# A hybrid attention and convolution trunk in float32: q, k and v projected 512 columns at a time, bias and scale at eviction

## The chip, the cores and the metric

The kernel runs on one core of one Trainium2 chip. The metric is the device time of one execution in microseconds, the median of three. In the profile PE is TensorE's matmul, PEld its weight load, DVE VectorE, ACT ScalarE, POOL GpSimd and SP SyncE. Line numbers such as L332 are those of the kernel before; the order lists of the changed kernel carry its own numbers.

## The reference, cut

Two layers over a sequence of 512 tokens of width 1024, all in float32. Each is a feed-forward half step, the mixer, a second feed-forward half step and a norm. The change lies in the mixer:

```python
def mixer(h, ...):
    z = h @ w_in + b_in
    q, k, v, glu_in, gates = jnp.split(z, [1536, 3072, 4608, 6656], axis=-1)
    shp = (B, S, 3, 8, 64)              # 3 groups of 8 heads of 64
    q = apply_rope(rmsnorm(q.reshape(shp), q_norm[:, None, :]), cos, sin)
    k = apply_rope(rmsnorm(k.reshape(shp), k_norm[:, None, :]), cos, sin)
    v = v.reshape(shp)
    for g, (window, dil) in enumerate(((128, 1), (512, 4), (2048, 16))):
        o, l = dilated_window_attn(q[:, :, g], k[:, :, g], v[:, :, g], dil, window // (2 * dil))
    ...                                  # groups weighted by softmax of l, projected
    y_conv = conv_module(glu_in, ...)    # GLU, depthwise conv of 31, LayerNorm, silu, projection
    g_attn, g_conv = jnp.split(jax.nn.sigmoid(gates), 2, axis=-1)
    return (g_attn * y_attn + g_conv * y_conv) @ w_out
```

## The kernel before

Every float32 product is made of three matmuls on operands split into their upper and lower 12 bits: upper by upper, upper by lower, lower by upper (L166 to L168, where a helper issues them). `stage` (L155 to L164) fetches weights by SP into a raw tile of [128, 1024] (512 KB, two buffers), ScalarE casts the upper part (`hi`, L161) and VectorE subtracts for the lower (`lo`, L162); hi and lo have four buffers each. Activations are kept split too, transposed, as xgh and xgl: eight tiles of [128 channels, 512 tokens], not yet divided by the row norm.

The mixer computes the GLU's input (ps_ga, ps_gg into u), then for each of three head groups and each of two halves of four heads: a chunk of 256 columns of q, one of k, one of v, and the attention of these heads (scores ps_S, transposed probabilities ps_T, output ps_pv). Then come the gates (ps_gc, ps_gA, 192 matmuls each), the depthwise convolution, its LayerNorm, and the projections ps_cp, of the attention, and of the output. The convolution is one multiplication (L543) and 30 multiply-adds (L549) on VectorE for each of eight channel tiles, 240 multiply-adds a layer. The LayerNorm takes the sum of the eight tiles (L555), its mean by a matmul with ones (ps_mu, L557), a copy (L559), eight subtractions (L562), squares (L193) and their sums (L197, ps_ss L202), the root (L207), a diagonal (L216) broadcast by ps_bc (L218), then multiplication (L567), Silu (L568) and a new split (zh L175, zl L176), whose tiles ps_cp reads.

`tokens_chunk` (L320 to L337) projects 256 columns with tokens on the partitions: two stages of four row blocks, and for each of four token tiles eight row blocks by three matmuls of 128x256 (L332 to L334) and a fourth kind (L336) that adds the bias: a row of three parts of the bias against a row of three parts of 1/r (rt3, made at L286 to L297, ps_rt at L291), since the division by the row norm r comes later. There are 18 chunks a layer. For q and k, ScalarE copies the two PSUM banks out (z, L374), squares 64 columns at a time with an accumulator (L377, 16 for each chunk), VectorE rotates (L379 to L381) and normalizes (small operations on [128, 16], L383 to L390), TensorE transposes (ps_qT) and ScalarE copies into qkT (L401). v is scaled by ScalarE at eviction (L412) and goes through DRAM to its order of positions.

A scheduler sets the order of each engine's instructions when the program is built; each engine works its list in order. `stage` is ranked 150 places early, and the LayerNorm is ranked ahead of the attention. PSUM has eight banks: two named mm (projections), one st, five at (attention, transposes). The pools of the mixer hold four qkT pairs and ten V tiles.

Of the kernel before, what the change touches and what calls it, by code (L numbers as in the profile page):

```python
# [32 lines left out]
CH = 256            # columns of q, k or v at a time: four heads  # L33
# [11 lines left out]
def trunk(ctx: ExitStack, tc: tile.TileContext, A: dict, out: bass.AP):  # L45
# [8 lines left out]
    def ps_mm(name):  # L54
        return psp.tile([P, S], F32, tag="mm", name=name, bufs=2)
# [17 lines left out]
    # input, natural layout  # L73
# [153 lines left out]
    def proj_cols(src, c0, rhs, nk, ps):  # L227
        """ps[j] = src[:, c0 + 128 j ..].T @ rhs, one or two tiles of columns."""
# [44 lines left out]
    def mixer(l, xg, R, rc, after):  # L273
# [5 lines left out]
        with ExitStack() as mx:  # L279
# [5 lines left out]
            # 1 / r as a row of three parts, and eps / r^2  # L285
            rr, rt = rc  # L286
            e4 = rp.tile([P, TT], F32, tag="e4", name=uniq("e4"))
            nc.vector.scalar_tensor_tensor(e4, rt, EPS, rt, op0=ALU.mult, op1=ALU.mult)
            ps = ps_st(uniq("ps_rt"))
            for tt in range(TT):  # L290
                nc.tensor.matmul(ps[:1, tt * P:(tt + 1) * P], rt[:, tt:tt + 1], ident, start=True, stop=True)  # L291
            rh, rl_ = slot("tmp", 7, F32R)[:1, :], slot("tmp", 7, F32R)[:1, :]
            nc.scalar.activation(rh, ps[:1, :], AF.Copy)
            nc.vector.tensor_sub(rl_, ps[:1, :], rh.bitcast(F32))
            rt3 = slot("rt3", 1, F32R)[:3, :]
            for i, t in enumerate((rh, rl_, rh)):
                nc.gpsimd.dma_start(rt3[i:i + 1, :], t)  # L297

# [487 lines left out]
```

## Time and profile before

| | |
|---|---|
| three runs | 2724.01, 2725.06, 2725.06 us |
| median | 2725.06 us |
| profiled execution, span from first to last instruction | 2723.4 us |
| TensorE matmul busy in it | 2704.4 us (99%), 14013 instructions |
| VectorE busy | 1536.0 us (56%) |
| ScalarE busy | 1148.1 us (42%) |
| GpSimd busy | 149.6 us (5%) |
| granted TensorE clock, mean | 0.998 |

Busy times are of one execution, and the profile gives that execution no time beside its span. A matmul's row lasts longer than the distance to the next one, as matmuls are pipelined; the distance is read from start times. Instructions of VectorE overlap a little in the same way. A share of the whole span says little here, since the mixers (about 471 to 887 us, and 1819 to 2234 us) load VectorE quite otherwise than the feed-forward steps.

### The profile page before, as it was taken

To read this page: it belongs to the slowest core of one execution; us is meant where nothing else is said; L and a number is where in the kernel's file an instruction comes from. 1 tells how busy PE (TensorE), PEld (TensorE's weight loads), DVE (VectorE), ACT (ScalarE), POOL (GpSimd) and SP (SyncE) were. 2 spreads that over 40 slices of the span, in tenths; PEclk is the share of its full clock that TensorE was granted. 3 is DMA by queue.
4 is the path that set the end of the run, shared out by engine and by line. 5 is a ranking of instruction groups with operands and counts; after the bars stand their busy time and mean duration, and the time that the engine had idled before them with its cause. 6 is when DMAs were issued, how large, how long until landed. Compare 5 with 4: busy or idle time off the path is not lost.

```text
span 2723.4 us, 35608 instructions
## 1 busy us (share of the span) xinstructions
PE 2704.4 (99%) x14013; PEld 2242.8 (82%) x14013; DVE 1536.0 (56%) x2543; ACT 1148.1 (42%) x2457; POOL 149.6 (5%) x275
## 2 busy tenths in 40 slices
PE   8999999999999999999999999999999999999998
PEld 6888888988887788888888888889888877888887
DVE  4443344888888754443454434458888876434432
ACT  5232232656677343232333222335567773322322
POOL 2000000111120000000000000001111200000000
PEclk9999999999999999999999999999999999999999
DMA  4232233223233323322333333322322333333322
GB/s 157 93 101 91 93 98 94 88 87 98 86 101 104 123 89 98 100 93 93 93 94 100 94 95 94 99 91 87 96 86 87 106 107 116 93 101 93 101 89 74
DMA packets 260455, 264.50 MB, mean 97 GB/s; under 512 B 12542, under 2 KB 251742, under 8 KB 260288
## 3 DMA queue, kind: packets, MB, share of 16 engines
q1 hardware_dynamic: 247488, 234.91, 27.9%
q0 software_dynamic: 12784, 27.32, 3.3%
q8 instruction: 110, 1.80, 0.3%
q14 instruction: 57, 0.47, 0.1%
q10 hardware_dynamic: 16, 0.00, 0.0%
HBM read 247.18 MB, written 14.99 MB: 96 GB/s over the span
## 4 chain that ended last, share of the span: by engine, by line
PE 97%; ACT 1%; DVE 1%; DMA 0%; issue 0%; SPq 0%; ACTq 0%
PE ps_n L332 6%; PE ps_d L167 6%; PE ps_d L166 6%; PE ps_d L168 6%; PE ps_a L167 6%; PE ps_b L166 6%; PE ps_a L168 6%; PE ps_b L168 6%; PE ps_b L167 6%; PE ps_a L166 6%; PE ps_n L333 5%; PE ps_n L334 5%; PE ps_n L336 2%; PE ps_pv L487 2%; PE ps_S L457 1%; PE ps_T L479 1%
## 5 line engine op out<-in xcount | busy, mean ns | idle before, releaser
L162 DVE TENSOR_TENSOR lo<-raw,hi 128x1024 fp32r<-128x1024 f32 (+1 forms) x448 | 539.4, 1204 | 797.1 <-ACT hi L161 795.6
L161 ACT ACTIVATE hi<-raw 128x1024 fp32r<-128x1024 f32 (+1 forms) x448 | 467.7, 1044 | 970.6 <-issue 353.8
L332 PE MATMUL ps_n<-hi,xgh 128*128 128x256 f32 x1152 | 343.5, 298 | 0.0
L549 DVE SCALAR_TENSOR_TENSOR cv<-u,cwc,cv 128x497 f32<-128x497 f32 (+14 forms) x480 | 335.7, 736 | 0.1
L333 PE MATMUL ps_n<-lo,xgh 128*128 128x256 f32 x1152 | 330.1, 287 | 0.0
L334 PE MATMUL ps_n<-hi,xgl 128*128 128x256 f32 x1152 | 328.6, 285 | 0.0
L168 PE MATMUL ps_d<-sh,lo 128*128 128x512 f32 x704 | 277.4, 394 | 0.0
L166 PE MATMUL ps_d<-sh,hi 128*128 128x512 f32 x704 | 277.4, 394 | 0.0
L167 PE MATMUL ps_d<-sl,hi 128*128 128x512 f32 x704 | 277.4, 394 | 0.0
L167 PE MATMUL ps_b<-xgl,hi 128*128 128x512 f32 x704 | 275.5, 391 | 0.0
L167 PE MATMUL ps_a<-xgl,hi 128*128 128x512 f32 x704 | 274.1, 389 | 0.1
L168 PE MATMUL ps_a<-xgh,lo 128*128 128x512 f32 x704 | 274.1, 389 | 0.0
L166 PE MATMUL ps_b<-xgh,hi 128*128 128x512 f32 x704 | 273.9, 389 | 0.0
L168 PE MATMUL ps_b<-xgh,lo 128*128 128x512 f32 x704 | 273.9, 389 | 0.0
L166 PE MATMUL ps_a<-xgh,hi 128*128 128x512 f32 x704 | 273.3, 389 | 0.3 <-ACT xgh L183 0.3
L332 PEld LDWEIGHTS ps_n<-hi,xgh 128*128 128x128 f32 x1152 | 219.4, 190 | 21.4 <-issue 2.8
L333 PEld LDWEIGHTS ps_n<-lo,xgh 128*128 128x128 f32 x1152 | 220.0, 191 | 3.9 <-issue 3.6
L334 PEld LDWEIGHTS ps_n<-hi,xgl 128*128 128x128 f32 x1152 | 219.9, 191 | 2.4 <-issue 2.1
L166 PEld LDWEIGHTS ps_d<-sh,hi 128*128 128x128 f32 x704 | 131.7, 187 | 32.6
L168 PEld LDWEIGHTS ps_d<-sh,lo 128*128 128x128 f32 x704 | 131.6, 187 | 32.6
L167 PEld LDWEIGHTS ps_d<-sl,hi 128*128 128x128 f32 x704 | 131.7, 187 | 32.6
L168 PEld LDWEIGHTS ps_b<-xgh,lo 128*128 128x128 f32 x704 | 132.2, 188 | 28.3 <-issue 1.0
(247 smaller groups left out, 4276.5 us busy)
## 6 DMA issues: line engine op xcount, KB each, us to landing
raw<-in_ffn_w_up_dram SPq DMA_DIRECT2D x176, 512.0 KB, 3.5
raw<-in_w_in_dram SPq DMA_DIRECT2D x136, 512.0 KB, 3.6
raw<-in_ffn_w_down_dram SPq DMA_DIRECT2D x76, 512.0 KB, 3.4
raw<-in_w_conv_proj_dram SPq DMA_DIRECT2D x16, 512.0 KB, 3.4
raw<-in_w_out_dram SPq DMA_DIRECT2D x16, 512.0 KB, 3.5
vd<-tmp POOLq DMA_DIRECT2D x24, 256.0 KB, 2.7
od<-ot POOLq DMA_DIRECT2D x24, 256.0 KB, 3.0
oin<-od POOLq DMA_DIRECT2D x24, 256.0 KB, 3.0
```

Of the source, the lines that this page charges most:

```text
L161: nc.scalar.activation(hi[:, :m], raw[:, :m], AF.Copy)
L162: nc.vector.tensor_sub(lo[:, :m], raw[:, :m], hi[:, :m].bitcast(F32))
L166: nc.tensor.matmul(ps, ah, bh, start=first, stop=False)
L167: nc.tensor.matmul(ps, ah, bl, start=False, stop=False)
L168: nc.tensor.matmul(ps, al, bh, start=False, stop=last)
L332: nc.tensor.matmul(o, xh[:, ts], wh, start=k == 0, stop=False)
L333: nc.tensor.matmul(o, xh[:, ts], wl, start=False, stop=False)
L334: nc.tensor.matmul(o, xl[:, ts], wh, start=False, stop=False)
L336: nc.tensor.matmul(o, rt3[:, ts], b3, start=False, stop=True)
L457: nc.tensor.matmul(pS[e][:, w * n + lo:w * n + hi], qT[hp, i, b * P:(b + 1) * P], kT[hp, i, k0 + lo:k0 + hi], start=True, stop=True)
L487: nc.tensor.matmul(pv[e * 64:(e + 1) * 64, i, b - b2, :], V[b + j][:, h * HD:(h + 1) * HD], PT[e][:, (nj * w + j) * P:(nj * w + j + 1) * P ...
L549: nc.vector.scalar_tensor_tensor(a[:, t0:t1], u[k][:, t0 + d:t1 + d], cw(l, j, k), a[:, t0:t1], op0=ALU.mult, op1=ALU.add)
```

## The change

A chunk is now 512 columns: 256 of q and 256 of k of the same four heads side by side, or 512 of v for a group's eight heads, so nine chunks a layer. It has four stages of two row blocks (for q and k two transfers of 256 KB into each raw tile), and thereby fills all four hi and lo buffers. The matmuls are 128x512, in two passes of two token tiles. The bias matmul, the row 1/r and its three-part tiles are gone: VectorE evicts each bank with one operation, times the row's scale plus the bias, which a POOL transfer has spread over all partitions. Squares are one ScalarE instruction of 128x512 for each token tile, and VectorE sums them by heads. Tables, qkT and the gates' tiles are merged to match; V is loaded for the eight heads of a group at once. PSUM has three mm banks and four at. In a group the two q-and-k chunks come first, then v, then the two halves' attention.

```diff
@@ tile pools
-        return psp.tile([P, S], F32, tag="mm", name=name, bufs=2)
+        return psp.tile([P, S], F32, tag="mm", name=name, bufs=3)
-        return psp.tile([P, S], F32, tag="at", name=name, bufs=5)
+        return psp.tile([P, S], F32, tag="at", name=name, bufs=4)
@@ stage
-            nc.sync.dma_start(raw[:, :m].rearrange("p (a n) -> p a n", a=a), src)
+            rv = raw[:, :m].rearrange("p (a n) -> p a n", a=a)
+            for i, src in enumerate(srcs):
+                nc.sync.dma_start(rv[:, :, i * n1:(i + 1) * n1], src)
@@ tokens_chunk
-                w = [stage(win[:, kk:kk + 4, c0:c0 + CH]) for kk in (0, 4)]
-                b3 = mp.tile([3, CH], F32R, tag="bias", name=uniq("bias"), bufs=2)
-                nc.gpsimd.dma_start(b3, bd[(l * 3 * AW + c0) // CH])
-                for tt in range(TT):
-                    ts = slice(tt * P, (tt + 1) * P)
-                    o = ps[tt // 2][:, (tt % 2) * CH:(tt % 2 + 1) * CH]
+                n = S // len(cols)
+                bias = mp.tile([P, S], F32, tag="bias", name=uniq("bias"), bufs=2)
+                for i, c0 in enumerate(cols):
+                    nc.gpsimd.dma_start(bias[:, i * n:(i + 1) * n], bass.AP(tensor=A["b_in"].tensor, offset=A["b_in"].offset + l * IN_W + c0, ap=[[0, P], [1, n]]))
+                w = [stage(*(win[:, kk:kk + 2, c0:c0 + n] for c0 in cols)) for kk in range(0, KD, 2)]
+                for t2 in range(0, TT, 2):
+                    ps = [ps_mm(uniq("ps_n")) for _ in range(2)]
                     for k in range(KD):
-                        wh, wl = w[k // 4][0][:, k % 4], w[k // 4][1][:, k % 4]
+                        wh, wl = w[k // 2][0][:, k % 2], w[k // 2][1][:, k % 2]
                         xh, xl = xg[k]
-                        nc.tensor.matmul(o, xh[:, ts], wh, start=k == 0, stop=False)
-                        nc.tensor.matmul(o, xh[:, ts], wl, start=False, stop=False)
-                        nc.tensor.matmul(o, xl[:, ts], wh, start=False, stop=False)
-                    # the bias, over the scale that the rows still lack
-                    nc.tensor.matmul(o, rt3[:, ts], b3, start=False, stop=True)
-                return ps
+                        for t in range(2):
+                            ts = slice((t2 + t) * P, (t2 + t + 1) * P)
+                            mm3(ps[t], xh[:, ts], xl[:, ts], wh, wl, k == 0, k == KD - 1)
+                    for t in range(2):
+                        yield t2 + t, ps[t], bias
@@ qk_chunk
-                for i in range(2):
-                    nc.scalar.activation(zt[i], ps[i], AF.Copy)
-                    for t in range(2):
-                        for h in range(UH):
-                            nc.scalar.activation(trash, four(zt[i])[:, t, h], AF.Square, accum_out=v[:, 2 * i + t, h:h + 1])
+                for tt, ps, bias in tokens_chunk((c0, AW + c0)):
+                    z = slot("sgc", 8, name="z")
+                    nc.vector.scalar_tensor_tensor(z, ps, rr[:, tt:tt + 1], bias, op0=ALU.mult, op1=ALU.add)
+                    sq = slot("tmp", 7, name="sq")
+                    nc.scalar.activation(sq, z, AF.Square)
+                    nc.vector.reduce_sum(v[:, tt, :], sq.rearrange("p (h d) -> p h d", d=HD), axis=AX.X)
@@ v_chunk
+                for tt, ps, bias in tokens_chunk((2 * AW + g * AOW,)):
+                    v = slot("tmp", 7)
+                    nc.vector.scalar_tensor_tensor(v, ps, rr[:, tt:tt + 1], bias, op0=ALU.mult, op1=ALU.add)
+                    nc.gpsimd.dma_start(vd[tt * P:(tt + 1) * P, :], v)
@@ the loop over groups
-                tq, tk = tables(g, 0), tables(g, 1)
+                tab = tables(g)
+                qkT = [qk_chunk(g, hh, tab) for hh in range(2)]
+                V = v_chunk(g)
                 for hh in range(2):
-                    qT = qk_chunk(g, hh, 0, tq)
-                    kT = qk_chunk(g, hh, 1, tk)
-                    V = v_chunk(g, hh)
-                    attend(g, hh, qT, kT, V)
+                    attend(g, hh, qkT[hh], V)
```

Three places of the order lists show what moves. On VectorE, early in the first layer's first q chunk, before:

```order
L549 SCALAR_TENSOR_TENSOR cv_7437<-u_2733,cwc,cv_7437 128x498
L549 SCALAR_TENSOR_TENSOR cv_7469<-u_2740,cwc,cv_7469 128x498
L549 SCALAR_TENSOR_TENSOR cv_7437<-u_2733,cwc,cv_7437 128x499
L379 TENSOR_TENSOR p_513_3297<-z_3293,tab_3165 128x8x32
L380 TENSOR_TENSOR p_513_3297<-z_3293,tab_3165 128x8x32
L549 SCALAR_TENSOR_TENSOR cv_7469<-u_2740,cwc,cv_7469 128x499
L549 SCALAR_TENSOR_TENSOR cv_7437<-u_2733,cwc,cv_7437 128x500
```

and VectorE at the same place of the changed kernel, where L516 is the convolution:

```order
L516 SCALAR_TENSOR_TENSOR cv_6198<-u_2707,cwc,cv_6198 128x502
L347 SCALAR_TENSOR_TENSOR z_3230<-ps_n_3180,rsr_2563,bias_3149 128x512
L516 SCALAR_TENSOR_TENSOR cv_6230<-u_2714,cwc,cv_6230 128x502
L347 SCALAR_TENSOR_TENSOR z_3240<-ps_n_3181,rsr_2563,bias_3149 128x512
L516 SCALAR_TENSOR_TENSOR cv_6198<-u_2707,cwc,cv_6198 128x503
L352 TENSOR_TENSOR p_510_3235<-z_3230,tab_3138 128x8x32
L353 TENSOR_TENSOR p_510_3235<-z_3230,tab_3138 128x8x32
L516 SCALAR_TENSOR_TENSOR cv_6230<-u_2714,cwc,cv_6230 128x503
L350 TENSOR_REDUCE ssh_3146<-sq_3232 128x8
```

The evictions of PSUM (L347) and the sums of squares (L350) now stand between the convolution's instructions.

On TensorE, at the end of a chunk and the start of the next, before:

```order
L332 MATMUL ps_n_3348<-hi_3356,xgh_2560 128x256
L333 MATMUL ps_n_3348<-lo_3357,xgh_2560 128x256
L334 MATMUL ps_n_3348<-hi_3356,xgl_2561 128x256
L336 MATMUL ps_n_3348<-bias_3361,rt_401_2600 128x256
L332 MATMUL ps_n_3521<-hi_3524,xgh_1981 128x256
L333 MATMUL ps_n_3521<-lo_3525,xgh_1981 128x256
```

and TensorE at such a place of the changed kernel:

```order
L157 MATMUL ps_n_3251<-hi_3174,xgh_2549 128x512
L158 MATMUL ps_n_3251<-lo_3175,xgh_2549 128x512
L159 MATMUL ps_n_3251<-hi_3174,xgl_2550 128x512
L157 MATMUL ps_n_3389<-hi_3362,xgh_1970 128x512
L157 MATMUL ps_n_3390<-hi_3362,xgh_1970 128x512
L158 MATMUL ps_n_3389<-lo_3363,xgh_1970 128x512
```

The bias matmul is gone, and two token tiles of the new chunk (3389 and 3390) run side by side.

On TensorE, around the broadcast ps_bc of the convolution's LayerNorm, before:

```order
L167 MATMUL ps_gA_7370<-xgl_2371,hi_7404 128x512
L168 MATMUL ps_gA_7370<-xgh_2370,lo_7405 128x512
L218 MATMUL ps_bc_7750<-dg_7745,ones 128x512
L166 MATMUL ps_gA_7370<-xgh_2465,hi_7404 128x512
L167 MATMUL ps_gA_7370<-xgl_2466,hi_7404 128x512
L168 MATMUL ps_gA_7370<-xgh_2465,lo_7405 128x512
L166 MATMUL ps_gA_7371<-xgh_1981,hi_7374 128x512
```

and TensorE there in the changed kernel:

```order
L158 MATMUL ps_gA_6133<-xgl_2550,hi_6165 128x512
L159 MATMUL ps_gA_6133<-xgh_2549,lo_6166 128x512
L193 MATMUL ps_ss_6497<-ones,sq_6467 128x1 x4
L209 MATMUL ps_bc_6511<-dg_6506,ones 128x512
L157 MATMUL ps_cp_6688<-zh_6515,hi_6691 128x512
L157 MATMUL ps_cp_6689<-zh_6515,hi_6691 128x512
L158 MATMUL ps_cp_6688<-zl_6516,hi_6691 128x512
```

The gate's matmuls that stood between the LayerNorm's matmuls and ahead of ps_cp have moved forward, and ps_ss, ps_bc and ps_cp follow one another.

## Rows read from the trace of the kernel before

**Rows 1.** The page: busy time (1) and the chain that ended last (4).

```profile
PE 2704.4 (99%) x14013; PEld 2242.8 (82%) x14013; DVE 1536.0 (56%) x2543; ACT 1148.1 (42%) x2457; POOL 149.6 (5%) x275
...
PE 97%; ACT 1%; DVE 1%; DMA 0%; issue 0%; SPq 0%; ACTq 0%
```

**Rows 2.** Busy by window: length, PE, PEld, DVE, ACT, POOL, clock, DMA share, GB/s.

```profile
470.90:844.60 373.70, 373.70 (x2708) 325.50 (x2707) 320.73 (x696) 247.59 (x819) 56.84 (x102) 1.00 0.30 91
...
1006.00:1370.00 364.00, 364.00 (x1594) 297.92 (x1593) 150.53 (x177) 113.18 (x140) 0.00 (x0) 1.00 0.31 96
...
1819.00:2192.10 373.10, 373.10 (x2705) 324.92 (x2705) 320.58 (x696) 247.00 (x819) 56.83 (x102) 1.00 0.30 91
```

**Rows 3.** Timeline of PE in the first q chunk: start, length, engine, line, operation.

```profile
471.15 0.28 PE L332 MATMUL ps_n<-hi,xgh 128*128 128x256 f32 x1
...
476.69 0.28 PE L332 MATMUL ps_n<-hi,xgh 128*128 128x256 f32 x1
...
477.29 0.28 PE L334 MATMUL ps_n<-hi,xgl 128*128 128x256 f32 x1
477.49 0.38 PE L336 MATMUL ps_n<-bias,rt 3*128 3x256 f32 x1
477.81 0.39 PE L332 MATMUL ps_n<-hi,xgh 128*128 128x256 f32 x1
```

**Rows 4.** The chain of waits around the row 1/r, layer 1.

```profile
402.35 0.96 PE ps_rt L291 x8
```

**Rows 5.** Timeline of DVE: the LayerNorm's eight subtractions.

```profile
846.34 4.90 DVE L562 TENSOR_TENSOR cv<-cv,tmp 128x512 f32<-128x512 f32 x8 [1.24 <-ACT tmp L559]
```

**Rows 6.** Groups by line, forms apart: count, busy us, mean ns, idle before.

```profile
L162 DVE TENSOR_TENSOR lo<-raw,hi 128x1024 fp32r<-128x1024 f32 x428 | 523.4, 1223 | 718.4 <-ACT hi L161 716.9
...
L535 DVE TENSOR_TENSOR sga<-ps_gA,R 128x512 f32<-128x512 f32 x16 | 10.9, 680 | 8.2 <-PE ps_gA L168 8.2
...
L618 DVE SCALAR_TENSOR_TENSOR sgc<-ps_cp,pcol,sgc 128x512 f32<-128x512 f32 x16 | 11.8, 747 | 8.8 <-PE ps_cp L168 8.7
...
L315 DVE SCALAR_TENSOR_TENSOR u<-tmp,bcol,tmp 128x512 f32<-128x512 f32 x16 | 11.9, 743 | 1.0 <-ACT hi L161 0.5
...
L543 DVE TENSOR_SCALAR cv<-u,cwc,pcol 128x512 f32<-128x512 f32 x16 | 8.1, 549 | 0.0
...
L388 DVE TENSOR_TENSOR ssh<-ssh,ny 128x16 f32<-128x16 f32 x24 | 4.1, 171 | 13.7 <-ACT ny L385 13.5
...
L161 ACT ACTIVATE hi<-raw 128x1024 fp32r<-128x1024 f32 x428 | 453.4, 1060 | 881.8 <-issue 337.5 <-PE ps_d L167 214.3 <-PE ps_a L167 90.4
```

**Rows 7.** Waits of DVE from 470 to 845: total us, times, longest.

```profile
DVE lo L162 <- ACT hi L161: 24.7, 19, 2.9
DVE p L379 <- ACT z L374: 10.5, 8, 2.2
DVE ssh L388 <- ACT ny L385: 6.7, 5, 1.9
```

**Rows 8.** Timelines of PE, ACT and DVE from ps_mu, then ps_cp by tile.

```profile
844.64 1.02 PE L557 MATMUL ps_mu<-tmp,ones 128*128 128x512 f32 x2
...
866.34 0.26 ACT L207 ACTIVATE rst<-ps_ss,epsc 128x4 f32<-128x4 f32 x1
...
866.85 0.87 DVE L216 TENSOR_SCALAR dg<-ident,rsr 128x128 f32<-128x128 f32 x4
...
879.31 0.80 ACT L568 ACTIVATE cv<-cv,pcol 128x512 f32<-128x512 f32 x1
880.01 0.62 ACT L175 ACTIVATE zh<-cv 128x512 fp32r<-128x512 f32 x1
...
L166 PE MATMUL ps_cp<-zh,hi x128: 387/389/504, 880.0 to 2277.6; 128*128 128x512 f32 x128
```

**Rows 9.** Busy by window at the end of the run, columns as in rows 2.

```profile
2713.00:2716.00 3.00, 1.73 (x13) 1.50 (x14) 1.44 (x3) 2.68 (x4) 0.00 (x0) 0.74 0.00 0
2716.00:2719.00 3.00, 2.29 (x11) 1.89 (x9) 1.56 (x3) 1.36 (x2) 0.00 (x0) 0.50 0.90 343
```

More of the change, by code (lines that the diff above doesn't have):

```diff
@@ L270, in ffn, with mixer @@
                     after(k, fp)
-    def mixer(l, xg, R, rc, after):
+    def mixer(l, xg, R, rr, after):
         win = A["w_in"][l].rearrange("(k p) n -> p k n", p=P)
@@ L283, in slot @@
                 return mp.tile([P, S], dt, tag=tag, name=uniq(name or tag), bufs=bufs)
[L286 to L289, printed above, removed]
-            for tt in range(TT):
[L291 to L297, printed above, removed]
             u = [None] * KD
@@ L384, in qk_chunk @@
+                nc.vector.tensor_scalar(v, v, 1.0 / HD, EPS, op0=ALU.mult, op1=ALU.add)
                 nc.scalar.activation(y, v, AF.Ln)
                 nc.scalar.activation(y, y, AF.Exp, scale=-0.5)
-                for i in range(2):
-                    nc.vector.tensor_add(p1[i], p1[i], p2[i])
                 nc.vector.tensor_mul(v, v, y)
@@ L390, in qk_chunk @@
                 nc.vector.scalar_tensor_tensor(rs, v, 1.5, y, op0=ALU.add, op1=ALU.mult)
-                for i in range(2):
-                    nc.vector.tensor_mul(four(p1[i]), four(p1[i]), rs[:, tts[i], :, None].to_broadcast([P, 2, UH, HD]))
-                for i in range(2):
+                for tt in range(TT):
+                    z = p1[tt].rearrange("p (h d) -> p h d", d=HD)
+                    nc.vector.tensor_mul(z, z, rs[:, tt, :, None].to_broadcast([P, 2 * UH, HD]))
                     pt = ps_at(uniq("ps_qT"))
@@ L404, in v_chunk @@
-            def v_chunk(g, hh):
-                ps = tokens_chunk(2 * AW + g * AOW + hh * CH)
-                vd = drp.tile([S, CH], F32, tag="vd", name=uniq("vd"))
-                for t2 in range(2):
+                        nc.tensor.transpose(pt[:, q * P:(q + 1) * P], p1[tt][:, q * P:(q + 1) * P], ident)
+                    dst = oT.rearrange("p q (r a) -> p q a r", r=dil)[:, :, tt * n:(tt + 1) * n, :]
+                    nc.scalar.activation(dst, pt.rearrange("p (q i r) -> p q i r", q=4, r=dil), AF.Copy)
@@ L456, in attend @@
                                 hp = slice(e * 64, e * 64 + 64)
[L457 removed]
+                                nc.tensor.matmul(pS[e][:, w * n + lo:w * n + hi], qkT[hp, i, b * P:(b + 1) * P], qkT[hp, 2 + i, k0 + lo:k0 + hi], start=True, stop=True)
                         PT = []
@@ L678, in trunk @@
         nxt, sq = [], [None]
-        mixer(l, xg, R, rc, collect("ffn2_norm", l, nxt, sq))
+        mixer(l, xg, R, rc[0], collect("ffn2_norm", l, nxt, sq))
         xg, rc, R = nxt, sq[1], sq[2]
```

95 lines of the change are left out of this document (37 added, 58 removed).

## The prediction, written before the run

> **What bounds the kernel now.** I read the busy shares first. TensorE is busy for 2704.4 of 2723.4 us and makes up 97% of the chain that ended last; VectorE is busy for 1536.0 us, 56% [rows 1]. But that share is a mean: the depthwise convolution's 240 multiply-adds a layer run on VectorE in the mixer, beside TensorE's projections and attention. So I then read that stretch alone, from the first matmul into ps_n (471.15) to the one into ps_mu (844.64): 373.5 us, TensorE without a gap, VectorE 320.73, ScalarE 247.59; the stretch of layer 2 reads the same [rows 2]. TensorE sets the time there, and VectorE has 53.0 us left in it. Whatever the change takes from TensorE in this stretch is worth its price only until VectorE is full.
>
> **What TensorE gives back, a layer.** (1) Matmuls of q, k and v: 1728 of 256 columns become 864 of 512. The old ones follow one another every 0.12 us (five steps from 476.69 to 477.29) [rows 3]; those of 512 columns in the FFN every 0.228 (364.00 / 1594) [rows 2]. 1728 x 0.12 - 864 x 0.228 = 207.4 - 197.0 = 10.4 us. (2) The 72 bias matmuls go. Around one, the next L332 starts 0.52 us after the last L334, and without it would start after 0.12 [rows 3]: 72 x 0.40 = 28.8 us. (3) The matmuls that made the row 1/r, once a layer: 0.96 us [rows 4]. (4) In the new order 142 of the 192 matmuls into ps_gA stand ahead of ps_mu, where 56 stood: 86 x 0.228 = 19.6 us come into the stretch from behind it. TensorE's need in the stretch: 373.5 - 10.4 - 28.8 + 19.6 = 353.9 us.
>
> **What VectorE takes on, a layer.** An instruction lasts about 0.08 us longer than the step to the next: eight of 0.68 take 4.90 us, so the step is (4.90 - 0.68) / 7 = 0.60 [rows 5]. Counts are those of the new order between the last u and the last add ahead of ps_mu. 24 evictions of z, scale and bias in one: the trace has this operation with a PSUM source, L618, 747 ns, a step of 0.67 [rows 6]: 16.1 us. 12 evictions of v: 8.0. 24 sums over squares (TENSOR_REDUCE 128x512, which the trace lacks): bounded by the cheapest and dearest 128x512 there, L543 with a step of 0.47 and L618 with 0.67; I take 0.60, that of L535, the plain two-operand form: 14.4 (11.3 to 16.1). The small operations on [128, 16] fall from 48 to 24 (L388, a step of 0.09): -2.2. Four more subtractions of weights (L162, 1.14) and three more evictions of gates (L535) come forward with the ps_gA matmuls: 4.6 + 1.8. Sum: +42.7 (39.6 to 44.4), so VectorE needs 320.7 + 42.7 = 363.4 us of work, 9.5 more than TensorE. **The bound changes hands.**
>
> For the eviction the rows of L618 and L315 say that a PSUM source costs 4 ns more than one in SBUF (747 against 743) [rows 6]. [...]
>
> **What is taken off ScalarE** costs and gives nothing: it is busy for 247.59 of 373.7 us [rows 2], so it is no bound, and loses the copies of z, the squares of 64 columns and the scaling of v. **DMA**: the weights of a q-and-k chunk come in two transfers for each buffer, the bytes unchanged at a DMA share of 0.30 [rows 2]; bias rows come spread over all partitions through POOL's queue, which is 5% busy [rows 1], and sit ahead of the chunk whose eviction reads them. I cost them at nothing, hidden by the chunk's own 21.9 us of matmuls (96 x 0.228); if that cover failed, the first eviction of each of 18 chunks would be late by a transfer.
>
> **Waits of the new bound.** VectorE idles 53.0 us in the stretch now. Of those, 24.7 are for the cast of weights that ScalarE does when TensorE releases a buffer, and 10.5 for z when TensorE ends a chunk [rows 7]: VectorE running ahead of TensorE, which stops once it is the one that is late. The remaining 17.8 come from the latency of attention and norm (6.7 of them for the inverse root) [rows 7], whose chains stay; I take 17.8. The new wait of TENSOR_REDUCE for ScalarE's square is covered in the list by two half-tile multiplications and a conv instruction, over 1 us; were it late, conv work and the next eviction would queue behind it. The attention has four PSUM banks for five: its next scores wait for a copy of the last, which costs TensorE from its 9.5 us of reserve before it costs VectorE. Bounds: 3, where conv instructions fill nearly everything, and 53.0, all of today's. The stretch: 363.4 + 17.8 = 381.2, or **+7.7 us**.
>
> **Behind ps_mu** TensorE had 136 gate matmuls to do, 31 us, and the LayerNorm ran beside them: from ps_mu at 844.64 to the first ps_cp at 880.0, 35.4 us [rows 8]. With 50 left (11.4 us), ahead of ps_ss in the new order, the LayerNorm's own chain sets the end: copy of the mean 1.7 (844.64 to 846.34), eight subtractions 4.9 [rows 5, 8]; on VectorE's queue seven adds of squares, two gates and three subtractions of weights, 4.2 + 1.2 + 3.4 [rows 6]; ps_ss 1.0, by the eight of ps_rt [rows 4], and ps_bc 1.0, by ps_mu's pair; from the root at 866.34 to the diagonal's end at 867.72, 1.4 [rows 8]; multiply 0.6, a cast of weights on ScalarE's queue 1.06 [rows 6], Silu 0.8, zh 0.6 [rows 8]. 21.9 us: **-13.5**.
>
> **Sum**: a layer 7.7 - 13.5 = -5.8; two layers -11.6; the row 1/r -1.9 in all; -13.5 us. The execution in the profile spans 2723.4, 1.7 us under the median 2725.06, and what lies around the two mixers stays: 2709.9 in its terms, **2711.6 us** against the median. Written with the wait w of a layer, the change is 2 (w - 23.6) - 1.9. What a measurement tells from no change is about 0.2%, 5.4 us: no change for w from 21.9 to 27.4.
>
> **Rivals.**
> *A, TensorE stays the bound.* If VectorE's added work fits into its 53 us of idle time after all, TensorE's saving shows whole: 2 x (10.4 + 28.8 + 0.96) = 80.3, 2644.8 us. For it: 42.7 is less than 53.0. Against: the gates pulled ahead and the waits that the chains force. Chance 0.07.
> *B, slower: the ring of weights holds one chunk.* Four buffers each of hi and lo held two chunks of 256; the first buffer of the next chunk came free a chunk ahead. Now a chunk fills all four. Its first buffer is released after 6 of the last 24 matmuls of the fourth token tile, which leaves 18 x 0.228 = 4.1 us for ScalarE's cast (1.06) and VectorE's subtraction (1.22), each in its queue [rows 6]: 1.8 us of slack, some three conv instructions. VectorE, full, is late with the subtraction, TensorE stands, and VectorE then stands for its z. It decides from w = 27.4 on, 9.6 us a layer above the forecast's, or 1.06 us at each of nine chunks. At 2.5 us each, where the longest wait for such a cast is now 2.9 [rows 7]: w = 17.8 + 22.5 = 40.3, 2 x 16.7 - 1.9 = +31.5, 2756.6 us. For it: two engines within 3% of each other, coupled by a ring of one. Against: the scheduler's list sets the subtraction ahead of conv work. Chance 0.28.
> *C, the clock.* [...] Chance 0.12; with w at 21.9 to 27.4 for other reasons 0.08 more.
> *D, the wide matmul brings nothing*, two times 0.12 as before: TensorE's need becomes 364.3, a us over VectorE's. That is inside the forecast, and its chance is in it.
>
> **How the numbers follow.** Forecast (VectorE bounds the stretch, w from 3 to 21.9) 0.45, A 0.07: faster 0.52. C and the middle: same 0.20. B: slower 0.28. The forecast's own low end is w = 3: 2725.06 - 43.1 = 2682.0; with the reduce at its lower bound 3.1 a layer less, 2675.8: low 2676. The high end is B's 2756.6, put at 2757, beyond which I leave 0.12.
>
> **What would show it.** VectorE busy near 363 us between ps_n and ps_mu in each layer and TensorE no longer at the full stretch; L347 near 747 ns; TENSOR_REDUCE between 550 and 750; ps_n matmuls 0.228 apart; 22 us from ps_mu to ps_cp. Wrong if the stretch gets shorter than 363 (A), if the largest of TensorE's waits is for lo or hi at a chunk's start (B), if the granted clock in the stretch falls under 0.97 (C).

## The result

The changed kernel takes 2702.22 us (median of four runs, 2699.16 to 2704.60) where the kernel before takes 2724.97 (four runs, 2724.01 to 2725.06): a ratio of 0.9917, 95% interval 0.9903 to 0.9931, 22.8 us less. Forecast were 2711.6 and faster, in a range of 2676 to 2757. The sign and the range held; the sum did not come about as it was written. Its profiled execution spans 2699.7 us and took 2701.68.

The page of the changed kernel, first its busy times, the clock in 40 slices, and the chain that ended last, the lines that answer to [rows 1]:

```profile
PE 2629.4 (97%) x12125; PEld 2133.9 (79%) x12125; DVE 1602.0 (59%) x2606; ACT 1005.0 (37%) x1568; POOL 110.7 (4%) x208
...
PEclk9999999998998999999999999999989989999999
...
PE 88%; DVE 9%; issue 1%; DMA 1%; ACT 1%; SPq 0%; POOL 0%; DVEq 0%; ACTq 0%; POOLq 0%
```

The clock row of the kernel before:

```profile
PEclk9999999999999999999999999999999999999999
```

TensorE is busy for 75.0 us less, but the run is only 22.8 shorter: VectorE now has 9% of the chain, and the clock, which stood at full in every slice before, has four 8s, two in each mixer. The 75.0 us are not yet the 80.3 that the prediction had TensorE give back. Some 17 of them lie outside the mixers, as the table below shows. In the two mixers, from the first ps_ga to the first ps_ap, TensorE's busy time falls from 1074.1 to 1016.5 us, by 57.6. There it now works for 55.9 us at a clock of 0.50; at full speed that work would take 28 us or more, so the work saved is between 57.6 and 85.6 us, an estimate.

The mixer by stretches, busy time of each engine as in [rows 2]: from the first ps_n to ps_mu, on to the first ps_cp, on to the first ps_ap in layer 1, and the first of them in layer 2:

```profile
466.40:841.10 374.70, 360.57 (x1870) 283.10 (x1869) 359.48 (x736) 180.46 (x381) 39.22 (x72) 0.98 0.33 100
1804.90:2178.10 373.20, 356.88 (x1858) 280.76 (x1857) 360.28 (x737) 187.63 (x387) 38.99 (x72) 0.98 0.34 102
841.10:866.30 25.20, 16.88 (x66) 12.04 (x64) 19.02 (x34) 15.62 (x24) 2.98 (x5) 0.82 0.38 122
866.30:927.10 60.80, 56.66 (x220) 43.31 (x221) 38.36 (x63) 20.05 (x29) 4.30 (x8) 0.85 0.31 95
```

and the last two of them in the kernel before:

```profile
844.64:880.00 35.36, 35.36 (x168) 28.30 (x166) 26.91 (x55) 24.27 (x35) 2.98 (x5) 1.00 0.35 109
880.00:930.80 50.80, 49.97 (x216) 37.69 (x217) 35.82 (x49) 18.91 (x26) 4.30 (x8) 1.00 0.43 135
```

The first stretch kept its length (373.5 before), with TensorE 14.1 us idle in it and VectorE 15.2. The second lost 10.2 us, and the third, which the prediction left alone, gained 10.0: TensorE is busy there for 6.7 us more (56.66 against 49.97) and idle for 3.3 more. From the start times of the first matmuls, the change of each stretch in layers 1 and 2:

| stretch | before | after, layer 1 / 2 | change | forecast a layer |
|---|---|---|---|---|
| first ps_ga to first ps_n | 78.2 | 77.0 / 77.0 | -1.2 / -1.2 | -0.96 |
| ps_n to ps_mu | 373.5 | 374.7 / 372.7 | +1.2 / -0.8 | +7.7 |
| ps_mu to ps_cp | 35.4 | 25.2 / 22.6 | -10.2 / -12.7 | -13.5 |
| ps_cp to ps_ap | 50.8 | 60.8 / 59.5 | +10.0 / +8.7 | 0 |
| sum of these, both layers | | | -6.2 | -13.5 (both layers) |
| all the rest (the spans differ by 23.7) | | | -17.5 | 0 |

Three quarters of the gain lie outside everything that the change rewrites. The group of the feed-forward's second matmul shows where, here in the kernel before

```profile
L166 PE MATMUL ps_d<-sh,hi 128*128 128x512 f32 x704 | 277.4, 394 | 0.0
```

and in the changed one:

```profile
L157 PE MATMUL ps_d<-sh,hi 128*128 128x512 f32 x704 | 274.1, 389 | 0.0
```

The same instruction is 5 ns shorter, and seven of its steps take 1.58 us where they took 1.63. From the first ps_d, at 257.9 in both kernels, to the first ps_ga 135.0 us became 131.5: 3.5 / 528 = 0.0066 us a matmul. ps_ap and ps_o did the same, 394 to 389; ps_a and ps_b were at 389 to 391 before and stay there. 2688 such matmuls by 0.0066 us are 17.7 us. Nothing in the code of these steps was changed.

### The profile page after: what moved, and what is told of

Its sections match the earlier page's. It is cut to its first block, busy times and chain, and to the rows that moved or that the text cites. A ratio compares the mean times of both kernels' runs of the same rounds, so it can differ in the third digit from the quotient of the medians.

```text
span 2699.7 us, 30972 instructions
## 1 busy us (share of the span) xinstructions
PE 2629.4 (97%) x12125; PEld 2133.9 (79%) x12125; DVE 1602.0 (59%) x2606; ACT 1005.0 (37%) x1568; POOL 110.7 (4%) x208
## 4 chain that ended last, share of the span: by engine, by line
PE 88%; DVE 9%; issue 1%; DMA 1%; ACT 1%; SPq 0%; POOL 0%; DVEq 0%; ACTq 0%; POOLq 0%
PE ps_a L159 6%; PE ps_a L158 6%; PE ps_b L157 6%; PE ps_d L159 6%; PE ps_b L158 6%; PE ps_b L159 6%; PE ps_d L158 6%; PE ps_d L157 6%; PE ps_a L157 6%; DVE cv L516 3%; PE ps_n L158 3%; PE ps_n L157 3%; PE ps_n L159 3%; PE ps_S L424 1%; PE ps_pv L454 1%
## 5 line engine op out<-in xcount | busy, mean ns | idle before, releaser
L516 DVE SCALAR_TENSOR_TENSOR cv<-u,cwc,cv 128x497 f32<-128x497 f32 (+14 forms) x480 | 334.9, 734 | 0.1
L158 PE MATMUL ps_n<-lo,xgh 128*128 128x512 f32 x576 | 229.1, 398 | 4.0 <-DVE lo L153 3.8
L159 PE MATMUL ps_n<-hi,xgl 128*128 128x512 f32 x576 | 225.4, 392 | 0.0
L157 PE MATMUL ps_n<-hi,xgh 128*128 128x512 f32 x576 | 215.8, 395 | 6.5 <-DVE tmp L379 4.3
L157 PEld LDWEIGHTS ps_a<-xgh,hi 128*128 128x128 f32 x704 | 132.1, 188 | 28.7 <-ACT xgh L174 1.2
L158 PEld LDWEIGHTS ps_b<-xgl,hi 128*128 128x128 f32 x704 | 132.2, 188 | 28.0 <-issue 0.7
L158 PEld LDWEIGHTS ps_a<-xgl,hi 128*128 128x128 f32 x704 | 132.2, 188 | 27.8 <-DVE xgl L175 0.5
L159 PEld LDWEIGHTS ps_a<-xgh,lo 128*128 128x128 f32 x704 | 132.2, 188 | 27.6 <-issue 0.2
```

Source lines behind the costliest of these rows:

```text
L157: nc.tensor.matmul(ps, ah, bh, start=first, stop=False)
L158: nc.tensor.matmul(ps, ah, bl, start=False, stop=False)
L159: nc.tensor.matmul(ps, al, bh, start=False, stop=last)
L516: nc.vector.scalar_tensor_tensor(a[:, t0:t1], u[k][:, t0 + d:t1 + d], cw(l, j, k), a[:, t0:t1], op0=ALU.mult, op1=ALU.add)
```

## Experiments

All times stand beside the kernel before on the same chip, 2724.8 to 2725.0 us. The two kernels with half the convolution, the one without bias matmuls and the two with pads ran once each, the others four to ten times. For each kernel the three stretches of the mixer (layer 1 / layer 2, us, from start times), and the time:

| kernel | ps_n to ps_mu | ps_mu to ps_cp | ps_cp to ps_ap | time |
|---|---|---|---|---|
| before | 373.5 / 373.5 | 35.4 / 35.3 | 50.8 / 50.8 | 2724.9 |
| before, 64 bytes higher | 372.9 / 372.9 | 35.4 / 35.3 | 50.8 / 50.9 | 2705.9 |
| changed | 374.7 / 372.7 | 25.2 / 22.6 | 60.8 / 59.5 | 2702.2 |
| changed, 64 bytes higher | 373.5 / 374.1 | 24.5 / 21.7 | 57.9 / 60.4 | 2705.1 |
| changed, idle matmuls | 374.0 / 374.2 | 24.4 / 24.4 | 61.5 / 61.6 | 2707.5 |
| changed, gates late | 367.7 / 371.8 | 32.2 / 33.0 | 59.7 / 56.9 | 2708.3 |
| changed, 256 columns | 373.1 / 380.1 | 31.6 / 34.9 | 58.5 / 57.3 | 2722.8 |
| changed, sums on ScalarE | 359.4 / 354.3 | 25.9 / 30.4 | 60.5 / 59.9 | 2678.4 |
| the same, 256 columns | 365.0 / 351.6 | 33.2 / 49.6 | 53.8 / 53.1 | 2693.0 |
| before, no bias matmuls | 350.5 / 350.4 | 29.6 / 29.6 | 60.5 / 58.1 | 2681.7 |

### Where the tiles lie

The change resized small tiles in a pool that lies below those of the feed-forward steps and the mixer (ssh, ny, rsh, e4), so all tiles above it moved: by the built programs' addresses the moving tiles of ps_d began at byte 134176 of a partition and now begin at 134496. Theory: that, and not the change's work, made them faster. The edit, in both kernels, adds 64 bytes below them and moves no instruction on any engine:

```diff
-  t = rp.tile([P, TT], F32, tag="t4", name=uniq("t4"))
+  t = rp.tile([P, TT], F32, tag="t4", name=uniq("t4"), bufs=4)
```

Expected of the kernel before:

> The kernel before with one small pool grown by 64 bytes a partition; no instruction and no order changes, but every tile of the feed-forward steps and of the mixer lies 64 bytes higher, as it does in the changed kernel. Theory (the matmuls of ps_d, ps_ap and ps_o became faster in the changed kernel only by where their moving tiles lie): they last 389 ns instead of 394, 0.0065 us a step less, 2688 of them, -17 us, about 2708 us; both stretches from ps_n to ps_mu stay at 373.5. Rival (they are faster because less goes on beside them): 2725 us, 394 ns.

Measured: 2705.88 us (2705.80 to 2706.02, ratio 0.9931, 0.9916 to 0.9946), and ps_d

```profile
L166 PE MATMUL ps_d<-sh,hi 128*128 128x512 f32 x704 | 273.9, 389 | 0.0
```

19.0 us without an instruction changed or put elsewhere in the order: the placing alone is shown to be worth that. Against this kernel the changed one is only 3.7 us shorter, and as the interval of each ratio is 0.14 to 0.15% (about 4 us) either way, that is hardly told from no change.

Expected of the changed kernel:

> The changed kernel with the same 64 bytes added, so that its tiles lie as those of the kernel before do within 128 bytes. Theory: ps_d, ps_ap and ps_o go from 389 to 394 ns, +17 us, about 2719 us, which leaves some -6 us for all that the change does to the work itself. Rival: 2702 us.

Measured: 2705.10 (2702.79 to 2706.75), only 2.9 us longer, where the theory had 2719. Its ps_d is slow in two of three forms:

```profile
L157 PE MATMUL ps_d<-sh,hi 128*128 128x512 f32 x704 | 277.4, 394 | 0.0
L159 PE MATMUL ps_d<-sh,lo 128*128 128x512 f32 x704 | 276.0, 392 | 0.0
L158 PE MATMUL ps_d<-sl,hi 128*128 128x512 f32 x704 | 273.2, 388 | 0.0
```

From the first ps_d to the first ps_ga it takes 132.7 us, where the changed kernel took 131.5: 1.18 / 528 = 0.0022 us a matmul, some 6 us over all 2688 (an estimate), of which the mixers gave half back. So the place of the moving tile within 128 bytes, which is here again what it was in the kernel before, does not settle it alone. Two more kernels move the four feed-forward steps by different amounts, the second with the weights moved too:

```diff
   with tc.tile_pool(name=uniq("ffn"), bufs=4) as fp:
+      if calls[0]:
+          nc.gpsimd.memset(fp.tile([P, 8 * calls[0]], F32, tag="pad", name=uniq("pad"), bufs=1), 0.0)
+      calls[0] += 1
```

> The kernel before with the pool of its four feed-forward steps begun 0, 32, 64 and 96 bytes a partition higher, one after the other; the mixers lie as before. Theory (the rate of a 128x512 matmul hangs on where its moving tile lies in SBUF): ps_d lasts 394 ns in the first step, 389 in the third, where the tiles lie as in the run that moved everything by 64 bytes; the second and fourth tell what the other two places are worth. About 2715 us if two of the four are fast. Rival (it hangs on the weights' or the norm's tiles, which moved by 64 bytes in that run too): 394 ns in all four.

> As the kernel with the four places of the feed-forward pool, with the weights' tiles and all behind them 64 bytes higher. If the distance between a moving tile and the weights counts: ps_d 394 ns in the first step again, 389 in the third, and ps_a and ps_b, whose moving tiles stay where they were while the weights move, leave 389. If the moving tile's own place counts: 389 in the first step, 394 in the third, ps_a and ps_b stay at 389.

Measured, ns of ps_d with the place of its moving tiles within 128 bytes of a partition:

| weights at | step 1 | step 2 | step 3 | step 4 | ps_a, ps_b (moving tiles at 96) |
|---|---|---|---|---|---|
| 96 | at 32: 394 | at 64: 396 | at 96: 389 | at 0: 395 | 389 to 394 |
| 32 | at 96: 394 | at 0: 396 | at 32: 390 | at 64: 395 | 394 to 400 |

The first kernel took 2721.6 us with one step of four fast; the second 2752.4, since ps_a and ps_b left 389 when only the weights moved. (The last column gives means of a step's groups; 22 of 24 lie at 389 to 391 in the first kernel, 23 of 24 at 394 to 398 in the second.) The distance counts: in these eight cases the matmul is fast only where moving tile and weights lie alike within 128 bytes. The changed kernel 64 bytes higher is the exception (weights at 96, moving tiles at 32, forms at 388 to 394). Within 128 bytes its distance is the same as that of the kernel before. Within 256 bytes, by the addresses of the built programs, it is not: there the moving tiles lie 64 bytes past the weights, and in the slow cases 64 before them, 32 before, or 32 past. No other run here has 64 past, so whether that place is a partly fast one stays untested.

### Which engine holds the stretch

Theory: VectorE. Rival: TensorE and the chains of attention. First 128 of 240 multiply-adds a layer are left out, in both kernels:

```diff
-                    if d == 0:
+                    if d == 0 or d % 2:
```

Expected of the changed kernel:

> The changed kernel with 16 of the convolution's 30 multiply-adds a channel tile left out, 128 of 240 a layer, 83 us of VectorE's work. Theory (VectorE is the bound of the mixer now): the time falls towards TensorE's need, by 40 to 75 us, to 2627 to 2660 us, and TensorE's gaps in the mixer nearly close. Rival (TensorE and the chains of attention still set the end): within 5 us of 2702.

Expected of the kernel before:

> The kernel before with the same 16 of 30 multiply-adds left out. Theory (TensorE is the bound there, without a gap): 2720 to 2726 us, as with the whole convolution, though VectorE loses 166 us of work in the two layers. Rival (VectorE's queue held TensorE back before too): 2700 us or less.

Measured: 2659.0 against 2702.2, and 2724.0 against 2724.8, both within what was expected. The kernel before doesn't notice 166 us less work on VectorE; the changed one loses 43.2 us. Its windows to the first ps_cp (ps_mu comes long before, since the convolution ends early) and on to ps_ap:

```profile
466.30:854.30 388.00, 373.50 (x1938) 292.98 (x1937) 304.62 (x661) 206.14 (x422) 41.98 (x77) 0.98 0.33 103
854.30:905.70 51.40, 51.40 (x218) 38.25 (x217) 32.56 (x44) 12.46 (x16) 4.30 (x8) 1.00 0.39 123
```

One part of the expectation failed: TensorE's gaps do not nearly close. Up to the first ps_cp it still idles 14.5 us (388.00 - 373.50), where the changed kernel has 22.5 (399.9 us, busy for 377.4). Of 83 us of VectorE's work taken out in a layer, 11.9 and 14.7 show up to the first ps_cp, and 9.3 and 6.4 in the stretch behind it. So VectorE's work holds part of the stretch, and most of what it lost there is not given back.

Then one part undone, the sums of squares back on ScalarE:

```diff
-  sq = slot("tmp", 7, name="sq")
-  nc.scalar.activation(sq, z, AF.Square)
-  nc.vector.reduce_sum(v[:, tt, :], sq.rearrange("p (h d) -> p h d", d=HD), axis=AX.X)
+  for h in range(2 * UH):
+      nc.scalar.activation(trash, z[:, h * HD:(h + 1) * HD], AF.Square, accum_out=v[:, tt, h:h + 1])
```

> The changed kernel with one part undone: the squares of q and k are again summed on ScalarE, 64 columns at a time with an accumulator, and the 24 sums a layer on VectorE go. VectorE loses 24 x 0.60 = 14.4 us a layer, ScalarE gains some 60 of the 195 that it idles in the stretch. Theory (VectorE bounds the stretch): 10 to 15 us less a layer, 2672 to 2682 us. Rival (the norm's chain gets longer by eight ScalarE pairs of 0.36 us a token tile, and the attention waits for it): 2700 us or more.

Measured: 2678.42 us (2676.31 to 2680.93; ratio to before 0.9832, 0.9816 to 0.9848), 23.8 less than the changed kernel. The norm's chain does get longer, as the rival has it (384 pairs of 254 and 188 ns on ScalarE), but VectorE's relief outweighs it:

```profile
466.50:825.90 359.40, 349.75 (x1838) 275.50 (x1836) 343.74 (x710) 224.74 (x739) 37.59 (x70) 1.00 0.33 104
```

VectorE's busy time fell by 15.7 us (359.48 to 343.74) and the stretch by 15.3. It lies in the range that the theory gave. Of the kernels that leave nothing out it is the fastest, and it beats both kernels of the comparison.

Then the headline of the change undone, in the changed kernel and in the one with sums on ScalarE: matmuls of 256 columns, left and right half of a bank in turn.

```diff
-  for k in range(KD):
-      wh, wl = w[k // 2][0][:, k % 2], w[k // 2][1][:, k % 2]
+  for c in (slice(0, CH), slice(CH, 2 * CH)):
+    for k in range(KD):
+      wh, wl = w[k // 2][0][:, k % 2, c], w[k // 2][1][:, k % 2, c]
...
-          mm3(ps[t], xh[:, ts], xl[:, ts], wh, wl, k == 0, k == KD - 1)
+          mm3(ps[t][:, c], xh[:, ts], xl[:, ts], wh, wl, k == 0, k == KD - 1)
```

> The changed kernel with its matmuls of q, k and v 256 columns wide again, the left and the right half of each bank one after the other; all else stays, the ring of four and the evictions too. TensorE gets 10.4 us more a layer, and the order of the list changes with it: 71 gate matmuls stand ahead of ps_mu instead of 142. Theory (VectorE bounds the stretch to ps_mu; the width of the matmuls is worth little beside it): the stretch stays within 370 to 376 us, ps_mu to ps_cp grows to 33 to 36 and ps_cp to ps_ap falls to about 51 with the clock at 1.0, 2695 to 2705 us. Rival (TensorE's time counts in full): 2 x 10.4 us more, 2723 us.

> The kernel with the squares summed on ScalarE, with matmuls of 256 columns. There VectorE and TensorE need nearly the same time in the stretch. Theory: TensorE bounds it again with the narrow matmuls, the stretch grows by 3 to 8 us a layer and what follows loses as much as in the kernel above: 2676 to 2690 us. Rival (TensorE's time counts in full): 2 x 10.4 more, 2699 us.

Measured: 2722.81 (2719.11 to 2728.17, ten runs), 20.6 more, and 2693.01 (2688.89 to 2694.80), 14.6 more. With the sums on ScalarE both the theory's 2676 to 2690 and the rival's 2699 were wrong; there the stretch from ps_mu to ps_cp grew most (49.6 us in layer 2). Without them the theory's 2695 to 2705 was wrong and the rival's 2723 right to the microsecond, though not by its mechanism: layer 1 takes 2.5 us more from ps_n to ps_ap, layer 2 17.5. In layer 2's stretch neither engine is full:

```profile
1809.20:2189.30 380.10, 359.06 (x2671) 323.81 (x2670) 355.13 (x730) 178.55 (x380) 40.07 (x74) 0.97 0.31 97
```

and what TensorE waits for is the ring of weights (waits of the whole run, total, times, longest):

```profile
PE ps_n L158 <- DVE lo L153: 18.0, 8, 3.2
...
PE ps_n L157 <- ACT hi L152: 6.1, 6, 2.9
```

against 3.8 and 1.1 in the changed kernel. So "VectorE bounds the stretch" is too simple. With 355 to 360 us of work on each of two engines, 14.4 us a layer taken from VectorE showed nearly whole (-23.8 in two layers), and 10.4 us a layer put on TensorE showed whole or more than half (20.6 and 14.6). That each engine waits for the other in short stretches is how I read this; no run takes work out of TensorE's list in the changed kernel (the gates held back, below, only move it). How much of the 20.6 us is the width itself and how much the other order that the scheduler made for it, these runs leave open.

### The bias matmuls alone

```diff
-                    nc.tensor.matmul(o, rt3[:, ts], b3, start=False, stop=True)
```

(and the row 1/r with it).

> The kernel before without the bias matmuls and the row 1/r that they read: the bias of q, k and v is left out, all else stays, chunks of 256 columns too. Theory (72 bias matmuls a layer at 0.40 us each, on the engine that sets the time, and VectorE with 53 us to spare in the stretch): 28.8 us a layer and 1.9 in all, 59.5 us less, 2665 us; the stretch from ps_n to ps_mu falls from 373.5 to about 345. Rival (the latency of attention on VectorE takes part of it up): 10 to 20 us a layer, 2685 to 2705 us.

Measured: 2681.7 us, 43.1 less, where theory had 2665 (a stretch of 345) and the rival 2685 to 2705: neither holds. The windows of its three stretches in layer 1:

```profile
469.50:820.00 350.50, 350.50 (x2691) 317.59 (x2691) 323.35 (x700) 248.74 (x824) 48.60 (x86) 1.00 0.32 100
820.00:849.60 29.60, 24.39 (x108) 19.04 (x106) 21.85 (x37) 19.51 (x28) 2.98 (x5) 0.95 0.37 119
849.60:910.10 60.50, 57.28 (x220) 43.42 (x221) 37.92 (x63) 19.77 (x29) 4.29 (x8) 0.85 0.33 105
```

Stretch and wait for ps_cp together lose 28.8 us (23.0 + 5.8), which is the forecast price of 72 bias matmuls, but the figures meet by chance: TensorE idles for 5.2 of the 29.6 us, and its busy time in the two falls by 34.0 (408.9 to 374.9), though beside the 72 bias matmuls only four others (ps_cT) no longer lie there. TensorE has no gap up to ps_mu, so what was freed there was filled with gate matmuls from behind (98 stand ahead of ps_mu, 56 before). But ps_cp to ps_ap grows by 9.7 and 7.3, at a clock of 0.85. The low clock has the same pattern as in the changed kernel: 0.50 from 846.9 to 857.2, and again near 878 and 885. What the changed kernel loses behind ps_cp is therefore had without the wide matmuls and the evictions: taking TensorE's filling out of the LayerNorm is enough.

### The stretch behind ps_cp

Theory: TensorE's pause ahead of ps_cp lowers the clock, and ps_cp pays. The first kernel fills the pause with matmuls that nobody reads:

```diff
+                pf = ps_mm(uniq("ps_fill"))
+                for _ in range(4):
+                    nc.tensor.matmul(pf, ones, cv[KD - 1], start=True, stop=True)
+                cols = sq.columns()
+                for _ in range(3):
+                    nc.tensor.matmul(pf, ones, sq.acc, start=True, stop=True)
...
```

> The changed kernel with seven idle matmuls of ones in each LayerNorm of the convolution (four behind the subtractions, three behind ps_ss), whose results nothing reads. Theory (TensorE's pause there lowers the granted clock, and the projection ps_cp pays): the clock of the 61 us from ps_cp to ps_ap rises from 0.85 to 0.95 or more, and the stretch falls from 60.8 to about 53; some 2 x 7 us less, about 2688 us. Rival (ps_cp is longer because its tiles z and the outputs of attention come late): no gain, 2702 to 2708 us with the idle matmuls' time.

Measured: 2707.46 (2706.76 to 2708.26), 5.2 more, where the theory had 2688; the rival's 2702 to 2708 holds.

```profile
841.60:866.00 24.40, 21.08 (x81) 13.66 (x79) 19.38 (x33) 17.10 (x25) 2.98 (x5) 1.00 0.39 123
866.00:927.50 61.50, 57.13 (x220) 43.34 (x221) 38.40 (x64) 20.09 (x29) 4.30 (x8) 0.86 0.29 94
```

The clock ahead of ps_cp went from 0.82 to 1.00, and behind it it fell as before (0.86 against 0.85). But the idle matmuls do not fill the pause: the last of them ends near 861.5, and the waits for z (total, times, longest, from 830 to 930) are what they were. In this kernel

```profile
PE ps_cp L157 <- ACT zh L166: 3.1, 1, 3.1
PE ps_cp L158 <- DVE zl L167: 1.9, 1, 1.9
```

and in the changed one

```profile
PE ps_cp L157 <- ACT zh L166: 2.9, 1, 2.9
PE ps_cp L158 <- DVE zl L167: 1.8, 1, 1.8
```

The fall of the clock moved behind the last idle matmul, from 857 to 867.5, and lasted to 874 as before. So this run leaves open whether a pause that is filled to its end would spare ps_cp. The second holds gates back (the new order of the gates' loop is left out here):

```diff
                 nc.scalar.activation(mu, ps, AF.Copy, scale=1.0 / D)
+                sg4 = mp.tile([P, 4, S], F32, tag="qk", name=uniq("sga"), bufs=2)
+                for k in range(4, KD):
+                    gate_a((k,), [ps_st(uniq("ps_gA"))], sg4)
...
-                rl = broadcast_psum(rsqrt_cols(sq.columns(), TT, 1.0 / D)[0], mp)
+                rl = broadcast_psum(rsqrt_cols(sq.columns(ps_at), TT, 1.0 / D)[0], mp, ps_at)
```

(`ps_at` gives the LayerNorm's sums and broadcast PSUM banks of the attention, in place of the one that the gates now use.)

> The changed kernel with the last four of eight gate tiles held back until the mean of the LayerNorm has been copied (they share its PSUM bank, and the LayerNorm's sums use another): 96 of the 192 matmuls into ps_gA behind ps_mu instead of 50. Theory (VectorE bounds the stretch to ps_mu, TensorE and its clock what follows): the stretch loses the VectorE work that goes with them, two gates and two or three subtractions of weights, 4 to 5 us, although 10.5 us of TensorE's work leave it; ps_mu to ps_cp takes 26 to 31 us; the clock stays at 1.0, and ps_cp to ps_ap takes 51 us: 8 to 10 us a layer less, 2682 to 2686 us. Rival (TensorE bounds the stretch): it falls by 10.5 us and what follows grows by as much, 2700 us.

Measured: 2708.31 (2707.32 to 2709.65), 6.1 more: neither the theory's 2682 to 2686 nor the rival's 2700. The stretch fell by 7.0 and 0.9, the wait for ps_cp grew by 7.0 and 10.4, and ps_cp to ps_ap stayed at 59.7 and 56.9. The clock was 0.50 from 832 to 842, around ps_mu, where TensorE now has a gap, and then 1.00 from 842 to 893, past the first ps_cp. Windows of five microseconds show that it then fell all the same:

```profile
885.00:890.00 5.00, 5.00 (x21) 3.48 (x19) 4.06 (x7) 1.58 (x2) 1.07 (x2) 1.00 0.61 180
890.00:895.00 5.00, 5.00 (x15) 2.99 (x15) 2.79 (x5) 0.00 (x0) 1.07 (x2) 0.85 0.74 229
895.00:900.00 5.00, 4.23 (x18) 2.74 (x17) 3.93 (x7) 1.69 (x2) 1.07 (x2) 0.81 0.40 116
900.00:905.00 5.00, 3.99 (x11) 2.88 (x10) 3.79 (x6) 0.63 (x1) 1.07 (x2) 0.53 0.50 161
```

What stands there is seen in TensorE's timeline in the changed kernel: start, length, line, tile.

```profile
869.36 0.80 PE L158 MATMUL ps_cp<-zl,hi 128*128 128x512 f32 x1 [1.80 <-DVE zl L167]
869.95 0.63 PE L159 MATMUL ps_cp<-zh,lo 128*128 128x512 f32 x1
...
893.44 0.49 PE L569 MATMUL ps_c<-tmp,sel 8*128 8x512 f32 x1
893.78 0.39 PE L570 MATMUL ps_c<-tmp,sel 8*128 8x512 f32 x1
894.10 0.50 PE L158 MATMUL ps_cp<-zl,hi 128*128 128x512 f32 x1
...
895.18 0.63 PE L158 MATMUL ps_cp<-zl,hi 128*128 128x512 f32 x1
895.61 0.63 PE L159 MATMUL ps_cp<-zh,lo 128*128 128x512 f32 x1
...
902.58 0.79 PE L157 MATMUL ps_cp<-zh,hi 128*128 128x512 f32 x1 [2.31 <-DVE oin L573]
```

There are two falls. The first begins at 857.0, while ps_ss waits for sq, and lasts to 874.1: ps_cp, waiting for its tiles z, runs at steps of 0.43 instead of 0.23. The second begins near 894.5, after a stretch in which the attention's ps_c, matmuls of 8 rows, stand by ones and twos between those of ps_cp, ends at 898, and comes again from 901.4 to 908.2, around a wait of 2.31 us for oin. In the kernel before the same matmuls ran at 1.00 throughout, though single ps_c stand between ps_cp there too (902.42, 903.52 and 906.44). With half the convolution, where z is there long before it is needed, no ps_cp waits in either layer, and layer 1 has 51.4 us at 1.00 (the window above), again with ps_c between; in layer 2 single ps_cp last 628 to 792 ns, as at the low clock above. So the 9 to 10 us are the low clock and the waits of a TensorE that meets ps_cp and ps_c without anything to put between. A TensorE that waits for sq and z goes with the first fall wherever it shows; sparse ps_c alone do not bring the second, which also came with the gates late, when there had been no fall from 842 on. What does bring it stays open, and the two were not tested apart.

## Why the prediction was right, and where it was not

**TensorE's saving** fits, as far as the rows can tell: ps_n's steps are 0.23 (466.44, 466.67, 466.90), and with the bias matmuls taken out alone TensorE's busy time up to ps_cp fell by 34.0 us a layer, where 28.8 were put. The busy time of the whole run, 75.0 us less, does not show the 80.3: some 17 of it are the shorter matmuls outside the mixers, and the 57.6 in the mixers were read at a lower clock (57.6 to 85.6 at full speed, the estimate above). The stretch's own need was put at 353.9 us and measured at 360.57 and 356.88.

**VectorE's load** held, slightly too high: +38.7 and +39.1 us between ps_n and ps_mu against 42.7, with the evictions at 742 ns (forecast 747) and the reduce at 674, a step of 0.59 where 0.60 was taken. Three more subtractions of weights came forward, not four. The two groups:

```profile
L347 DVE SCALAR_TENSOR_TENSOR z<-ps_n,rsr,bias 128x512 f32<-128x512 f32 x48 | 35.4, 742 | 2.6 <-PE ps_n L159 2.6
L350 DVE TENSOR_REDUCE ssh<-sq 128x8 f32<-128x512 f32 x48 | 32.4, 674 | 0.0
```

An eviction from PSUM costs VectorE no more than the same operation from SBUF: 742 ns, against 743 of L315 before and 747 of L292 in the changed kernel.

**The change of the bound** held in kind: VectorE idles 15.2 and 12.9 us in the stretch (forecast 17.8), and taking its work away shows (-23.8 for the sums, -43.2 for half the convolution) where it did not before (-0.8). In part only: of the 166 us of half the convolution three quarters did not show. The step said more than was so: TensorE's idle 14.1 us is not a reserve. The narrow matmuls, which by the forecast's 9.5 us of reserve should have cost about nothing, cost 20.6.

**The wait behind ps_mu** was forecast at 21.9 us and measured at 25.2 and 22.6. Of the 3.3 us of layer 1, 1.9 lie in TensorE's own part of the chain, at the low clock: ps_ss took 1.84 us and ps_bc 2.05, each put at 1.0. Another 1.6 lie ahead of ps_ss, which starts 17.0 us behind ps_mu where the terms of the sum make 15.4.

```profile
858.03 1.84 PE L193 MATMUL ps_ss<-ones,sq 128*128 128x1 f32 x8 [3.94 <-DVE sq L188]
861.44 2.05 PE L209 MATMUL ps_bc<-dg,ones 128*128 128x512 f32 x2 [1.57 <-DVE dg L207]
```

**Two terms were missing**, and they are larger than the forecast gain. "What lies around the two mixers stays" was wrong twice. ps_cp to ps_ap grew by 10.0 and 8.7 us: two falls of the clock and the waits between them, which no term of the sum has; rival C, the clock, held a chance of 0.12. And the rest of the run shrank by 17.5 us through the new places of tiles, which no step of the working looked at: a change to tile sizes was costed by its instructions alone. Without that the change is worth 3.7 us, so that the forecast of "faster" came true, and came near, is luck: it rests on a term that it did not contain. By the mixers alone (-6.2 us) it would stand at the edge of no change.

**The rivals.** A (TensorE stays the bound) falls with the two idle times. B (the ring of one chunk) does not show in the changed kernel, where TensorE waits 3.8 us for lo in the whole run, but appears as soon as the matmuls are narrow (18.0). C, the clock: low at the run's end before [rows 9], it now falls in the mixers too, at the end of group 0's attention (0.50 from 656 to 673 in layer 1, 1994 to 2011 in layer 2) and around ps_cp, and the mean went from 0.998 to 0.984. What the first of them cost the stretch is not shown, since VectorE is busy there throughout (17.00 of 17 us). The falls at 656 and 857 come where TensorE idles or has little to do: it is busy for 0.88 of the 4 us before 656 and for 0.10 of the 3 us before 857. At 894 the profile has TensorE busy (24.00 of 24 us from 870 on), so idle time alone does not explain that fall. D falls: the wide matmul's step is what was forecast (0.23 us).

## What to carry to other kernels

When an edit resizes or removes any tile, compare the addresses of the untouched hot tiles before crediting the edit: a 64-byte shift was worth 19.0 us here and the change itself some 3.7. Work taken from the bounding engine may have been the filling that hid another chain; look at what stood between the matmuls of the next dependent stage and price its absence with the clock (10.0 and 8.7 us from ps_cp to ps_ap here). When two engines end up within a few per cent of each other, as here with 355 to 360 us each, do not call either the bound without a run: unload the one that can hand work to an idle third, as here VectorE's sums to ScalarE (-23.8 us).

## What the runs showed of the hardware

A 128x512 matmul of these split operands lasts 389 to 391 ns or 394 to 398 (means of a step's groups, all but three of 72 in the two kernels with pads; 0.0066 us a step from 389 to 394) depending on where its moving tile lies relative to its weights in SBUF: fast in the cases with equal places within 128 bytes, slow where it lies 32 or 64 bytes before the weights or 32 past them, with one run, 64 past, that mixes both (388 to 394). TensorE's granted clock fell to 0.50 not only after idle time (at 857 us, TensorE busy for 0.10 of the 3 us before) but also in a stretch where the profile has TensorE busy throughout, with 8-row matmuls between the full ones (at 894 us, busy for 24.00 of 24 us before); in the kernel before, such a stretch ran at 1.00 (900 to 907 us, busy for 7.00 of 7).
